# A row-wise logsumexp: nearly all row sums moved to VectorE, the late ones by halves, and a shorter first load

## The chip, the cores and the metric

The kernel runs on one core of a Trainium2 chip. The metric is device time in microseconds (us), the median of several executions.

## The reference

```python
# x: (32, 512, 1024) float32; axis: -1
def reference(x, axis):
    x_max = np.max(x, axis=axis, keepdims=True)
    return (x_max.squeeze(axis) + np.log(np.sum(np.exp(x - x_max), axis=axis))).astype(np.float32)
```

That is 16384 rows of 1024 numbers, 67.1 MB, each read once. The kernels leave out the maximum (the inputs are standard normal draws, so the exponentials do not overflow) and compute log(sum(exp(x))).

## The kernel before

Each of the 128 partitions gets 128 rows, which arrive in 17 loads into a ring of 51 rows. A "row" below means one row in every partition, 512 KB in all. ScalarE (ACT) takes the exponential. The sum of a row is made in one of two ways: VectorE (DVE) sums several rows after a large exponential, or ACT's own accumulator sums a single row. The list says how many rows each load has, and how many of them DVE sums.

```python
CHUNKS = [
    (4, 1), (15, 11), (16, 10), (16, 15), (16, 0), (14, 0), (12, 9), (9, 5), (7, 5), (5, 4),
    (4, 3), (3, 0), (2, 2), (2, 2), (1, 0), (1, 0), (1, 0),
]
RING_ROWS = 51
LN_AT = 5
# ...
    load(0)                          # issued ahead of the start barrier
    n_early = len(body.instructions)
# ...
    for i, (r, n_dve) in enumerate(CHUNKS):
        if i:
            load(i)                  # waits until the ring slots it overwrites are free
        # ...
        nc.scalar.wait_ge(landed[i], 16)
        if n_dve:
            nc.scalar.activation(out=ring[:, s : s + n_dve], in_=ring[:, s : s + n_dve], func=Exp
            ).then_inc(act_done, 1)
            # ...
            nc.vector.reduce_sum(out=sums[:, row : row + n_dve], in_=ring[:, s : s + n_dve], axis=AX
            ).then_inc(dve_done, 1)
        for j in range(n_dve, r):    # one row at a time, summed by ACT's accumulator
            nc.scalar.activation(out=ring[:, s + j], in_=ring[:, s + j], func=Exp,
                accum_out=sums[:, row + j : row + j + 1]).then_inc(act_done, 1)
        # ...
    take_logs(logged, NB, dves, acts)        # logarithm of the 61 sums still open
    nc.scalar.wait_ge(act_done, acts)
    nc.scalar.dma_start(out=out_v, in_=res).then_inc(stored, 16)
```

The softmax here doesn't subtract the row's maximum and nothing guards it: scores larger than these inputs give would overflow.

Of the kernel before, what the change touches and what calls it, by code (L numbers as in the profile page):

```python
# [1 line left out]

# [4 lines left out]



CHUNKS = [  # L10
    (4, 1), (15, 11), (16, 10), (16, 15), (16, 0), (14, 0), (12, 9), (9, 5), (7, 5), (5, 4),
    (4, 3), (3, 0), (2, 2), (2, 2), (1, 0), (1, 0), (1, 0),
]
RING_ROWS = 51

LN_AT = 5


@with_exitstack
def kernel(  # L20
    ctx: ExitStack,
    tc: tile.TileContext,
    x: bass.AP,
    axis: bass.AP,
    out: bass.AP,
):
    nc = tc.nc
    P = nc.NUM_PARTITIONS

    assert axis in (-1, len(x.shape) - 1), f"only last-axis reduction supported, got {axis}"  # L30

    x_flat = x.flatten_outer_dims()
    N, D = x_flat.shape
    assert N % P == 0
    NB = N // P
    assert sum(r for r, _ in CHUNKS) == NB

    fp32 = mybir.dt.float32
    Exp = mybir.ActivationFunctionType.Exp
    Ln = mybir.ActivationFunctionType.Ln  # L40
    AX = mybir.AxisListType.X

    x_v = x_flat.rearrange("(p t) d -> p t d", p=P)
    out_v = bass.AP(tensor=out.tensor, offset=out.offset, ap=[[NB, P], [1, NB]])

    ring = nc.alloc_sbuf_tensor("ring", [P, RING_ROWS, D], fp32).ap()
    sums = nc.alloc_sbuf_tensor("sums", [P, NB], fp32).ap()
    res = nc.alloc_sbuf_tensor("res", [P, NB], fp32).ap()

    landed = [nc.alloc_semaphore(f"landed{i}") for i in range(len(CHUNKS))]  # L50
    act_done = nc.alloc_semaphore("act_done")
    dve_done = nc.alloc_semaphore("dve_done")
    stored = nc.alloc_semaphore("stored")
    used = sorted(sem.num for sem in [*landed, act_done, dve_done])
    assert used == list(range(used[0], used[0] + len(used)))


    hook = nc.pop_inst_callback()
    symbolic, nc._always_lower_symbolic_ap = nc._always_lower_symbolic_ap, False


    place = []
    row = slot = 0
    for r, _ in CHUNKS:
        if slot + r > RING_ROWS:
            slot = 0
        place.append((slot, row))
        slot += r
        row += r



    busy = [(0, 0)] * RING_ROWS
    acts = dves = 0

    def load(i):
        (s, row), r = place[i], CHUNKS[i][0]
        act_wait = max(a for a, _ in busy[s : s + r])
        dve_wait = max(d for _, d in busy[s : s + r])
        if dve_wait:  # L80
            nc.sync.wait_ge(dve_done, dve_wait)
        if act_wait:
            nc.sync.wait_ge(act_done, act_wait)
        nc.sync.dma_start(out=ring[:, s : s + r], in_=x_v[:, row : row + r]).then_inc(
            landed[i], 16
        )

    def take_logs(lo, hi, dve_wait, act_wait):
        nonlocal acts
        nc.scalar.wait_ge(act_done, act_wait)  # L90
        nc.scalar.wait_ge(dve_done, dve_wait)
        nc.scalar.activation(out=res[:, lo:hi], in_=sums[:, lo:hi], func=Ln).then_inc(  # L92
            act_done, 1
        )
        acts += 1

    body = nc.main_func.blocks[-1]
    assert not body.instructions
    load(0)
    n_early = len(body.instructions)  # L100

    nc.scalar.preload_act_table_set("natural_log_exp_and_others")  # L102

    logged = 0
    done_before = [(0, 0)]
    for i, (r, n_dve) in enumerate(CHUNKS):
        if i:
            load(i)
        s, row = place[i]
        if i == LN_AT:  # L110
            logged = row
            take_logs(0, logged, *done_before[i])
        nc.scalar.wait_ge(landed[i], 16)
        if n_dve:
            nc.scalar.activation(  # L115
                out=ring[:, s : s + n_dve], in_=ring[:, s : s + n_dve], func=Exp
            ).then_inc(act_done, 1)
            acts += 1
            nc.vector.wait_ge(act_done, acts)
            nc.vector.reduce_sum(  # L120
                out=sums[:, row : row + n_dve], in_=ring[:, s : s + n_dve], axis=AX
            ).then_inc(dve_done, 1)
            dves += 1
            for j in range(n_dve):
                busy[s + j] = (0, dves)
        for j in range(n_dve, r):
            nc.scalar.activation(  # L127
                out=ring[:, s + j],
                in_=ring[:, s + j],
                func=Exp,  # L130
                accum_out=sums[:, row + j : row + j + 1],
            ).then_inc(act_done, 1)
            acts += 1
            busy[s + j] = (acts, 0)
        done_before.append((dves, acts))

    take_logs(logged, NB, dves, acts)
    nc.scalar.wait_ge(act_done, acts)
    nc.scalar.dma_start(out=out_v, in_=res).then_inc(stored, 16)


    nc.scalar.sem_clear(range(used[0], used[-1] + 1))


    first = nc.main_func.blocks[0]
    head, work = first.instructions, body.instructions
    end = next(k for k, i in enumerate(head) if i.opcode == "UnconditionalBranch")
    head, tail = head[:end], head[end:]
    for ins in work[:n_early]:
        at = next(  # L150
            k for k, i in enumerate(head) if i.engine == ins.engine and i.opcode == "Drain"
        )
        head.insert(at, ins)
    first.instructions = head + work[n_early:] + tail
    body.instructions = []

    nc._always_lower_symbolic_ap = symbolic
    nc.push_inst_callback(hook)


    tc.close()
    tc.compile()
    nc.gpsimd.wait_ge(stored, 16)
    nc.gpsimd.sem_inc(stored, -16)


# [1 line left out]
_INS = ['x', 'axis']  # L168
_OUTS = [((32, 512), 'float32')]

_NUMBERS = {'axis': -1}


# [26 lines left out]
```

## Time and profile before

| | before |
|---|---|
| time, median | 163.45 us |
| span of the profiled run | 161.4 us |
| ACT busy | 124.1 us (77%) |
| DVE busy | 72.9 us (45%) |
| share of 16 load engines taken by the loads | 97.0% |
| last share of the last load lands | 158.21 us |
| result stored | 161.35 us |

The first thing to ask of a table like this is whether the busiest resource has holes. ACT at 77% has them, ahead of each of the first five loads (until 83.84 us). The loads at 97% have none between the first packet and the last. The last two rows of the table are landing records of the trace: a load is carried by 16 engines, and counts as landed when the last of the 16 shares is in. Their difference, 3.14 us, is called the tail below. It holds the last exponential, the last logarithm and the store.

### The profile page before, as it was taken

How to read it: one execution, taken by the hardware profiler on the slowest of the kernel's cores; microseconds unless marked ns; L12 is line 12 of the kernel's file. 1: busy time of each engine (PE TensorE's matmuls, PEld its weight loads, DVE VectorE, ACT ScalarE, POOL GpSimd, SP SyncE). 2: the span in 40 equal slices, each digit the busy share in tenths (PEclk: the TensorE clock that was granted, in tenths of full speed). 3: DMA queues.
4: the chain of work that ended last, by engine and by line, in shares of the span. 5: the costliest groups of instructions: out<-in, count | busy, mean ns of one | idle time of the engine just before them, and what ended most of it. 6: DMA issues, size and time to landing. Idle time of an engine off the chain costs nothing.

```text
span 161.4 us, 212 instructions
## 1 busy us (share of the span) xinstructions
DVE 72.9 (45%) x11; ACT 124.1 (77%) x136; POOL 0.2 (0%) x4
## 2 busy tenths in 40 slices
DVE  0030000029960699000799920000004999799874
ACT  3190006997089980999429999999999999999995
POOL 0000000000000000000000000000000000000000
DMA  7999799989989989989989999999899999999990
GB/s 264 499 487 442 335 442 520 422 357 520 422 357 520 422 357 520 422 357 520 422 353 426 457 455 422 390 463 475 347 439 434 433 441 402 431 418 416 420 394 24
DMA packets 2593, 67.18 MB, mean 416 GB/s; under 512 B 288, under 2 KB 416, under 8 KB 800
## 3 DMA queue, kind: packets, MB, share of 16 engines
q1 hardware_dynamic: 2448, 67.11, 97.0%
q10 hardware_dynamic: 144, 0.07, 0.1%
q14 instruction: 1, 0.01, 0.0%
HBM read 67.11 MB, written 0.07 MB: 416 GB/s over the span
## 4 chain that ended last, share of the span: by engine, by line
ACT 52%; DMA 38%; DVE 7%; issue 1%
DMA ring<-in_x_dram 38%; ACT ring L127 30%; ACT ring L115 22%; DVE sums L120 7%; ACT res L92 0%
## 5 line engine op out<-in xcount | busy, mean ns | idle before, releaser
L120 DVE TENSOR_REDUCE sums<-ring 128x5 f32<-128x5120 f32 (+8 forms) x11 | 72.9, 6648 | 86.1 <-ACT ring L115 86.0
L115 ACT ACTIVATE ring<-ring 128x5120 f32<-128x5120 f32 (+8 forms) x11 | 59.3, 5395 | 29.6 <-DMA ring<-in_x_dram 29.6
L127 ACT ACTIVATE ring<-ring 128x1024 f32<-128x1024 f32 x61 | 63.4, 1041 | 5.3 <-DMA ring<-in_x_dram 5.3
L127 ACT ACTIVATION_READ_ACCUMULATOR ring<-ring 128x1 f32 x61 | 11.4, 187 | 0.0
L102 ACT ACT_TABLE_LOAD x1 | 1.3, 1283 | 0.8 <-PEq L181 0.8
L92 ACT ACTIVATE res<-sums 128x67 f32<-128x67 f32 (+1 forms) x2 | 0.5, 256 | 0.1
L181 POOL MEMSET const-bfloat16-1.0<- 128x1 bf16 x1 | 0.1, 101 | 0.0
L181 POOL MEMSET const-uint8-127<- 128x1 uint8 x1 | 0.1, 101 | 0.0
L181 POOL MEMSET const-float32-0.0<- 128x1 f32 x1 | 0.1, 98 | 0.2 <-issue 0.2
L181 POOL MEMSET const-float32-1.0<- 128x1 f32 x1 | 0.1, 98 | 0.0
## 6 DMA issues: line engine op xcount, KB each, us to landing
ring<-in_x_dram SPq DMA_DIRECT2D x1, 7680.0 KB, 24.9
ring<-in_x_dram SPq DMA_DIRECT2D x1, 7168.0 KB, 36.0
ring<-in_x_dram SPq DMA_DIRECT2D x1, 6144.0 KB, 21.6
ring<-in_x_dram SPq DMA_DIRECT2D x1, 4608.0 KB, 32.1
ring<-in_x_dram SPq DMA_DIRECT2D x2, 2048.0 KB, 26.3
ring<-in_x_dram SPq DMA_DIRECT2D x1, 3584.0 KB, 40.2
ring<-in_x_dram SPq DMA_DIRECT2D x1, 2560.0 KB, 44.4
ring<-in_x_dram SPq DMA_DIRECT2D x2, 1024.0 KB, 46.0
```

Of the source, the lines that this page charges most:

```text
L92: nc.scalar.activation(out=res[:, lo:hi], in_=sums[:, lo:hi], func=Ln).then_inc(act_done, 1)
L102: nc.scalar.preload_act_table_set("natural_log_exp_and_others")
L115: nc.scalar.activation(out=ring[:, s : s + n_dve], in_=ring[:, s : s + n_dve], func=Exp).then_inc(act_done, 1)
L120: nc.vector.reduce_sum(out=sums[:, row : row + n_dve], in_=ring[:, s : s + n_dve], axis=AX).then_inc(dve_done, 1)
L127: nc.scalar.activation(out=ring[:, s + j], in_=ring[:, s + j], func=Exp, accum_out=sums[:, row + j : row + j + 1],).then_inc(act_done, 1)
L181: nc = _bacc.Bacc("TRN2", target_bir_lowering=False, num_devices=1)
```

## The change

The intent was to take work off ACT. A row that ACT sums itself costs it about 0.19 us more than its part in a large exponential (1.04 us start to start against 0.853 in the trace before). DVE gets 119 of 128 rows instead of 67. To keep DVE from being late at the end, 15 late rows are summed by halves: one instruction adds the two halves of a row and accumulates the result, so it is an instruction of 512 columns instead of 1024. The last four rows keep ACT's accumulator, which now writes to a tensor in PSUM instead of SBUF, where the ring lies. The first load has two rows instead of four, and two loads are issued ahead of the barrier. The trace before shows one fetch of instructions inside the span (q14, 8192 bytes in 335 ns at 89.07 us); with fewer instructions on ACT, it was to go.

```diff
 CHUNKS = [
-    (4, 1), (15, 11), (16, 10), (16, 15), (16, 0), (14, 0), (12, 9), (9, 5), (7, 5), (5, 4),
-    (4, 3), (3, 0), (2, 2), (2, 2), (1, 0), (1, 0), (1, 0),
+    (2, 2, 1, False), (15, 15, 1, False), (14, 14, 1, False), (16, 16, 2, False),
+    (16, 16, 2, False), (14, 14, 2, False), (14, 11, 2, False), (10, 10, 2, False),
+    (8, 6, 1, False), (6, 6, 1, True), (4, 4, 1, True), (3, 3, 1, True), (2, 2, 1, True),
+    (1, 0, 1, False), (1, 0, 1, False), (1, 0, 1, False), (1, 0, 1, False),
 ]                                  # rows, rows for DVE, pieces, by halves
-LN_AT = 5
+LN_AT = 7
+LN_LAG = 1
+LATE = 4
 ...
+    late = nc.alloc_psum_tensor("late", [P, 512], fp32).ap()
 ...
     load(0)
+    load(1)
 ...
+        if i == len(CHUNKS) - 1:
+            take_logs(logged, late_row, sums[:, logged:late_row], *done_before[-LATE])
 ...
+            if by_halves:
+                for j in range(lo, hi):
+                    nc.vector.tensor_tensor_reduce(
+                        out=ring[:, s + j, : D // 2],
+                        in0=ring[:, s + j, : D // 2],
+                        in1=ring[:, s + j, D // 2 :],
+                        scale=1.0, scalar=0.0, op0=Add, op1=Add,
+                        accum_out=sums[:, row + j : row + j + 1],
+                    ).then_inc(dve_done, 1)
 ...
-                accum_out=sums[:, row + j : row + j + 1],
+                accum_out=total(row + j),          # PSUM for the last four rows
 ...
-    take_logs(logged, NB, dves, acts)
+    take_logs(late_row, NB, late[:, : NB - late_row], dves, acts)
```

More of the change, by code (lines that the diff above doesn't have):

```diff
@@ L35 @@
     NB = N // P
-    assert sum(r for r, _ in CHUNKS) == NB
+    assert sum(r for r, *_ in CHUNKS) == NB
     fp32 = mybir.dt.float32
@@ L40 @@
     Ln = mybir.ActivationFunctionType.Ln
+    Add = mybir.AluOpType.add
     AX = mybir.AxisListType.X
@@ L63 @@
     row = slot = 0
-    for r, _ in CHUNKS:
+    for r, *_ in CHUNKS:
         if slot + r > RING_ROWS:
@@ L74, with cuts @@
     acts = dves = 0
+    def cuts(n, parts):
+        ends = [-(-n * k // parts) for k in range(parts + 1)]
+        return [(lo, hi) for lo, hi in zip(ends, ends[1:]) if lo < hi]
     def load(i):
@@ L86, in load, with take_logs @@
         )
-    def take_logs(lo, hi, dve_wait, act_wait):
+    def take_logs(lo, hi, src, dve_wait, act_wait):
         nonlocal acts
@@ L91, in take_logs, with total @@
         nc.scalar.wait_ge(dve_done, dve_wait)
-        nc.scalar.activation(out=res[:, lo:hi], in_=sums[:, lo:hi], func=Ln).then_inc(
-            act_done, 1
-        )
+        nc.scalar.activation(out=res[:, lo:hi], in_=src, func=Ln).then_inc(act_done, 1)
         acts += 1
+    late_row = place[-LATE][1]
+    assert not any(n_dve for _, n_dve, _, _ in CHUNKS[-LATE:])
+    def total(t):
+        return late[:, t - late_row : t - late_row + 1] if t >= late_row else sums[:, t : t + 1]
     body = nc.main_func.blocks[-1]
@@ L105 @@
     done_before = [(0, 0)]
-    for i, (r, n_dve) in enumerate(CHUNKS):
-        if i:
+    for i, (r, n_dve, parts, by_halves) in enumerate(CHUNKS):
+        if i > 1:
             load(i)
@@ L110 @@
         if i == LN_AT:
-            logged = row
-            take_logs(0, logged, *done_before[i])
+            logged = place[i - LN_LAG][1]
+            take_logs(0, logged, sums[:, :logged], *done_before[i - LN_LAG])
+        if i == len(CHUNKS) - 1:
+            take_logs(logged, late_row, sums[:, logged:late_row], *done_before[-LATE])
         nc.scalar.wait_ge(landed[i], 16)
-        if n_dve:
+        for lo, hi in cuts(n_dve, parts):
             nc.scalar.activation(
-                out=ring[:, s : s + n_dve], in_=ring[:, s : s + n_dve], func=Exp
+                out=ring[:, s + lo : s + hi], in_=ring[:, s + lo : s + hi], func=Exp
             ).then_inc(act_done, 1)
@@ L119 @@
             nc.vector.wait_ge(act_done, acts)
-            nc.vector.reduce_sum(
-                out=sums[:, row : row + n_dve], in_=ring[:, s : s + n_dve], axis=AX
-            ).then_inc(dve_done, 1)
-            dves += 1
-            for j in range(n_dve):
-                busy[s + j] = (0, dves)
+            if by_halves:
[4 more added lines that the diff above has]
+                        in1=ring[:, s + j, D // 2 :],
+                        scale=1.0,
+                        scalar=0.0,
+                        op0=Add,
+                        op1=Add,
+                        accum_out=sums[:, row + j : row + j + 1],
+                    ).then_inc(dve_done, 1)
+                    dves += 1
+                    busy[s + j] = (0, dves)
+            else:
+                nc.vector.reduce_sum(
+                    out=sums[:, row + lo : row + hi], in_=ring[:, s + lo : s + hi], axis=AX
+                ).then_inc(dve_done, 1)
+                dves += 1
+                for j in range(lo, hi):
+                    busy[s + j] = (0, dves)
         for j in range(n_dve, r):
```

## The prediction

> **What bounds the kernel now.** I read the page's slices and DMA queues first, because a kernel that reads 67 MB once can end no earlier than its last byte.
>
> ```profile
> DMA  7999799989989989989989999999899999999990
> q1 hardware_dynamic: 2448, 67.11, 97.0%
> q14 instruction: 1, 0.01, 0.0%
> ```
>
> The load queue is busy from the second slice to the last but one, with no hole; q14 is one fetch of instructions. The windows of the last microseconds show when it stops (columns: stretch, length, DVE, ACT, POOL busy, clock, DMA share, GB/s):
>
> ```profile
> 156.00:157.00 1.00, 1.00 (x2) 1.00 (x2) 0.00 (x0) 1.00 1.01 406
> 157.00:158.00 1.00, 1.00 (x1) 1.00 (x3) 0.00 (x0) 1.00 0.32 127
> 158.00:159.00 1.00, 1.00 (x1) 1.00 (x3) 0.00 (x0) 1.00 0.00 0
> ```
>
> In the trace's landings the last of the 16 shares of the last load arrives at 158.21 us; call this T. Then the chain of waits (start, length, what):
>
> ```profile
> 0.78 24.87 DMA ring<-in_x_dram
> 25.67 9.60 ACT ring L115
> 35.29 11.90 DVE sums L120
> 47.21 36.61 DMA ring<-in_x_dram
> 83.84 10.56 ACT ring L127 x21
> ...
> 159.28 0.19 ACT ring L127
> 159.50 0.25 ACT res L92
> ```
>
> By shares it says ACT 52%, DMA 38%, which invites one to relieve ACT. That is the trap: the chain goes through ACT because ACT never pauses after 83.84, but the loads never pause either. The step through DVE at 35.29 is the release of a ring slot; the load that it frees is issued at 47.21 and the queue still holds 17 us of work. So two limits coincide: the stream ends at T, and ACT reaches the last row 0.13 us later (the last exponential starts at 158.34). After T come exponential and accumulator read (to 159.47), logarithm (to 159.75), store (161.35); the span is 161.4 us, and the time, 163.45 us, is 2.05 above it.
>
> The stream has a simple law. The trace gives the median packet (one partition's rows of a load) as 161 ns for 1 row, 311 for 2, 611 for 4, 2267 for 15, 2420 for 16. Each of 16 engines carries eight per load: 8 x 2267 ns = 18.14 us against 18.13 between the first two landings; 8 x 2420 = 19.36 against 19.36 between the next two but one. The line through them is 10.5 ns a packet plus 150.6 ns a row, so a load costs 0.084 + 1.205 us a row. Costs of the engines, by form:
>
> ```profile
> L115 ACT ACTIVATE ring<-ring 128x11264 f32<-128x11264 f32 x1 | 9.6, 9589 | 14.0 <-DMA ring<-in_x_dram 14.0
> L127 ACT ACTIVATE ring<-ring 128x1024 f32<-128x1024 f32 x61 | 63.4, 1041 | 5.3 <-DMA ring<-in_x_dram 5.3
> L127 ACT ACTIVATION_READ_ACCUMULATOR ring<-ring 128x1 f32 x61 | 11.4, 187 | 0.0
> L120 DVE TENSOR_REDUCE sums<-ring 128x11 f32<-128x11264 f32 x1 | 11.9, 11885 | 25.4 <-ACT ring L115 25.4
> ```
>
> Start to start, an exponential of n rows costs 0.853n + 0.10 us (25.67 to the next instruction at 35.17: 9.50), a row with its own accumulator 1.04 (8.50 to 9.54). A VectorE sum of n rows takes 1.067n + 0.15 (11.885), about 0.09 of it hidden behind the next one (two of 2.28 us merge to 4.48). All three stay under the stream's 1.21 us a row.
>
> [...]
>
> **The change, part by part.**
>
> *First load of two rows, second issued before the barrier.* The stream now starts at an effective 2.62 us (7.52 landed, less 8 x 0.611). It still carries 128 rows in 17 loads, so by the law it ends where it ended: 2.62 + 17 x 0.084 + 128 x 1.205 = 158.3. Two rows last 2.5 us, and the second load is queued before the first byte moves (packets begin at 1.00 us), so no hole opens. ACT starts at about 5.1 rather than 7.5, into idle time. Worth 0, give or take 0.2 us.
>
> *The rows move to VectorE.* ACT sheds the accumulator cost on 52 of 61 rows, some 52 x 0.19 = 10 us less work, all of it ahead of waits for loads. DVE gets 119 rows instead of 67. Does it return slots in time? The tightest is load 4, which reuses the slots of loads 0 and 1. Load 1 lands at 5.1 + 18.14 = 23.3; its exponential ends at 36.2, its sum (15 x 1.067 + 0.15) at 52.4. The stream runs dry at 23.3 + 16.95 + 19.36 = 59.6. Slack 7.2 us, and an issue needs about 1.0 (0.00 to 1.00). Stepping the same sums on, load 5 is released at 67.5 against 79.0, load 6 at 84.7 against 95.9, load 7 at 103.3 against 112.9, load 8 at 110.8 against 125.0; later loads have more. No hole.
>
> *Half sums late.* An estimate from the reduce's own fixed costs: 512/0.96 = 0.533, about 0.06 start to start[...]: 0.65 us instead of 1.067. On 15 rows that saves 6 us of DVE work. Whether it is needed is seen backward from T. Loads of 6, 4, 3, 2 rows land at T-16.3, T-11.3, T-7.7, T-5.2. Their exponentials end at T-11.0, T-7.5, T-4.8, T-3.0. DVE, which carries a small queue from load 6 (done 130.1, load 7 at 141.0, load 8 at 147.5, that is T-10.8), then needs 6 x 0.65 to T-6.9, 4 x 0.65 to T-4.3, 3 x 0.65 to T-2.3, 2 x 0.65 to about T-1.0.
>
> *The tail on ACT.* Four single rows land at T-3.9, T-2.6, T-1.3, T. ACT, free at T-3.0, needs 1.04 each: T-2.0, T-0.9, T+0.1; rounding and a late start of the chunks make this T+0.1 to T+0.3. The logarithm of 47 sums now comes here, about 0.2 start to start (100.60 to 100.79 in the mid one). So the last exponential starts near T+0.4, against T+0.13 before: +0.3. The final logarithm is of 4 values instead of 61, 57/1.2 = 47 ns less[...]. Store unchanged.
>
> *Instruction fetch.* One packet of 335 ns on one of 16 engines goes. The shares of a load landed 0.84 us apart before it (82.97 to 83.81) and 0.83 after (114.47 to 115.30), so it did not delay the slowest engine: 0.
>
> Sum: stream 0, tail +0.3 - 0.1 = +0.2. 163.45 + 0.2 = about 163.6 us.
>
> **The rivals.**
>
> *The half sums run at half rate.* 1024/0.96 + 0.12 = 1.19 us a row. From T-10.8, 15 rows end at T+7.1; the logarithm of 47 waits, and then exponential, logarithm and store follow: +7.2 us, 170.7. [...]Against it: [...]that halving would have no sense for whoever tuned this. At 0.80 us a row, by the same sum, DVE ends at T+1.2 and the time is some 164.8.
>
> *A wait on slots takes the place of ACT's load.* Whole sums free slots late (52.4 instead of 47.2 for load 4). The 7.2 us of slack speak against it; if DVE were slower than the reduce shows, each microsecond past 59.6 less an issue time would be one of the total.
>
> *Relieving ACT gains.* If the chain's 52% were what sets the end, 10 us less would give 154. The stream's end at T forbids it: even with ACT done at once, only 0.13 us of lag could go. The gain can be no more than that plus the fetch's 0.3, or 163.0.
>
> *A faster start.* If smaller first packets shorten the start (the first packets took 1.0 to 1.5 us instead of 0.61), the whole stream shifts, by up to perhaps 0.4: 163.1.
>
> **Range and chances.** Stream and start give 0.3 either way, the tail 0.2; a half sum of 0.70 to 0.80 adds up to 1.2. Range 162.9 to 164.6, with most of what is outside on the slow side. A gain of 2% needs 160.2, before the stream's end plus its tail: 1%. A loss of 2% needs 166.7, which only half rate or a hole in the stream gives: 9%. Within 2%: 90%.
>
> **What would show it.** The chain should become almost all DMA until its last 2 us; ACT idle ahead of every load until about 142; the last landing within 0.3 of 158.2; the half sum with its read near 0.65 us start to start; the DVE's last one ended before the logarithm of 47; the last exponential 0.3 to 0.5 after T; no instruction packet inside the span. I am wrong if the slices of the load queue show a hole, if a half sum takes over 0.72 (then DVE ends after the third single row), or if the last landing moves by more than 0.4.

Its sum came to 163.45 + 0.3 - 0.1 = about 163.6 us. Of the 0.1, 47 ns stand as an estimate: 57 columns of the last logarithm at 1.2 columns a ns, the rate of ACT's exponentials in the trace before (13.00 us for 15 rows, 1.90 for 2). The other 50 ns or so were a gain assumed for PSUM; the kernel before has no tensor there. Without it the sum is about 163.7.

The 0.65 us of a half sum came from 0.533 + 0.06 + a term of about 0.06 for reading the accumulator. The 0.96 columns a ns are the rate of the reduce in the trace before (16.15 us for 15 rows, 5.48 for 5), and the first 0.06 is its fixed 0.15 less the 0.09 hidden behind the next one. The 0.12 in the rival's 1.19 us is the sum of the same two terms. That a sum of two inputs keeps the rate of the reduce was the estimate, and half rate a guess against it: the trace before has no such instruction.

## The result, and the profile after

The changed kernel is correct and takes 163.34 us (163.19 to 163.75, six runs) against 163.45 us (163.22 to 163.53, six runs). The ratio is 0.9998, 95% interval 0.9985 to 1.0011: the same. A ratio here is the mean time of one kernel's fast runs over the mean of the other's fast runs of the same rounds, so it is not quite the ratio of the medians quoted.

ACT's work fell from 124.1 to 115.1 us, DVE's rose from 72.9 to 121.4, and the time did not move. The page's slices and queues after the change:

```profile
DMA  7999799999989989989999999999999999999990
q1 hardware_dynamic: 2448, 67.11, 96.9%
```

The stream of loads still has no hole, and the line for the fetch of instructions (q14) is gone. The windows around its end, with the columns of the prediction's fence:

```profile
156.00:157.00 1.00, 0.77 (x4) 1.00 (x3) 0.00 (x0) 1.00 0.99 397
157.00:158.00 1.00, 0.00 (x0) 1.00 (x3) 0.00 (x0) 1.00 0.23 90
158.00:159.00 1.00, 0.00 (x0) 1.00 (x4) 0.00 (x0) 1.00 0.00 0
```

The stream stops in the same microsecond as before. The last share lands at 158.17 us against 158.21, and the tail is 3.12 us against 3.14. DVE is idle from 156.77 on. The chain of waits (start, length, what):

```profile
0.42 22.91 DMA ring<-in_x_dram
...
36.39 16.17 DVE sums L155
...
52.58 26.41 DMA ring<-in_x_dram
...
158.22 0.24 ACT res L105
158.46 1.01 ACT ring L162 x2
...
159.50 0.17 ACT res L105
```

This chain misleads in the same way as the one before. It passes through a DVE sum of 16 us because that sum released a ring slot at 52.58. But the load released there landed only at 78.99, behind a queue that did not run dry until 59.64. Time in which a released load waits behind other loads is shown as if the release had mattered. The costs of the engines, by form (busy us, then mean ns of one):

```profile
L135 ACT ACTIVATE ring<-ring 128x8192 f32<-128x8192 f32 x4 | 27.9, 7022 | 12.6 <-DMA ring<-in_x_dram 12.6
...
L142 DVE CUSTOM_DVE_ANT_0 ring<-ring 128x512 f32<-128x512 f32 x15 | 9.3, 689 | 0.0
...
L142 DVE DVE_READ_ACCUMULATOR2_ANT sums<- 128x1 f32 x15 | 1.3, 84 | 0.0
```

And the end of the timeline (start, length, engine, line, instruction):

```profile
148.10 0.08 DVE L142 DVE_READ_ACCUMULATOR2_ANT sums<- 128x1 f32 x1
148.10 0.69 DVE L142 CUSTOM_DVE_ANT_0 ring<-ring 128x512 f32<-128x512 f32 x1
148.72 0.08 DVE L142 DVE_READ_ACCUMULATOR2_ANT sums<- 128x1 f32 x1
...
156.68 0.09 DVE L142 DVE_READ_ACCUMULATOR2_ANT sums<- 128x1 f32 x1
...
157.22 1.05 ACT L162 ACTIVATE ring<-ring 128x1024 f32<-128x1024 f32 x1
...
158.22 0.24 ACT L105 ACTIVATE res<-sums 128x47 f32<-128x47 f32 x1
158.35 1.05 ACT L162 ACTIVATE ring<-ring 128x1024 f32<-128x1024 f32 x1
159.30 0.17 ACT L162 ACTIVATION_READ_ACCUMULATOR ring<-ring 128x1 f32 x1
159.50 0.17 ACT L105 ACTIVATE res<-late 128x4 f32<-128x4 f32 x1
```

The reader should see three things. The read of the accumulator (84 ns) starts together with the next half sum (148.10), so it adds nothing, and a half sum costs about 0.61 us start to start. The DVE's last one is done at 156.77, 1.45 us before the logarithm of 47 sums. And that logarithm takes 0.13 us of ACT (158.22 to 158.35) just before the last exponential.

### The profile page after: what moved, and what is told of

It is laid out like the page before. It is cut to its first block, busy times and chain, and to the rows that moved or that the text cites. A ratio compares the mean times of both kernels' runs of the same rounds, so it can differ in the third digit from the quotient of the medians.

```text
span 161.3 us, 146 instructions
## 1 busy us (share of the span) xinstructions
DVE 121.4 (75%) x44; ACT 115.1 (71%) x40; POOL 0.2 (0%) x4
## 4 chain that ended last, share of the span: by engine, by line
DMA 45%; ACT 28%; DVE 25%; issue 0%; SPq 0%
DMA ring<-in_x_dram 45%; DVE sums L155 25%; ACT ring L135 24%; ACT ring L162 4%; ACT res L105 0%; SPq L97 0%
## 5 line engine op out<-in xcount | busy, mean ns | idle before, releaser
L155 DVE TENSOR_REDUCE sums<-ring 128x8 f32<-128x8192 f32 (+6 forms) x14 | 112.2, 8071 | 35.4 <-ACT ring L135 35.4
L135 ACT ACTIVATE ring<-ring 128x8192 f32<-128x8192 f32 (+8 forms) x18 | 104.3, 5837 | 43.3 <-DMA ring<-in_x_dram 43.3
L162 ACT ACTIVATE ring<-ring 128x1024 f32<-128x1024 f32 x9 | 9.3, 1043 | 0.0
L142 DVE CUSTOM_DVE_ANT_0 ring<-ring 128x512 f32<-128x512 f32 x15 | 9.3, 689 | 0.0
L162 ACT ACTIVATION_READ_ACCUMULATOR ring<-ring 128x1 f32 x9 | 1.6, 175 | 0.0
L142 DVE DVE_READ_ACCUMULATOR2_ANT sums<- 128x1 f32 x15 | 1.3, 84 | 0.0
L105 ACT ACTIVATE res<-sums 128x77 f32<-128x77 f32 (+1 forms) x2 | 0.5, 248 | 0.0
```

What stands on the lines that cost most here:

```text
L105: nc.scalar.activation(out=res[:, lo:hi], in_=src, func=Ln).then_inc(act_done, 1)
L135: nc.scalar.activation(out=ring[:, s + lo : s + hi], in_=ring[:, s + lo : s + hi], func=Exp).then_inc(act_done, 1)
L142: nc.vector.tensor_tensor_reduce(out=ring[:, s + j, : D // 2], in0=ring[:, s + j, : D // 2], in1=ring[:, s + j, D // 2 :], scale=1.0, scal ...
L155: nc.vector.reduce_sum(out=sums[:, row + lo : row + hi], in_=ring[:, s + lo : s + hi], axis=AX).then_inc(dve_done, 1)
```

## The experiments

The theory: the stream of loads fixes the end, ACT and DVE both lie beside it with known slack, and the small pieces of the tail cancel. The rivals: the engines set the pace (so relieving one should gain, or loading the other should cost at once), or slot waits or the start shape the stream. Nine kernels tell these apart, and two runs repeat. Each edit is against the changed kernel.

The table gathers the trace records on which the readings rest (us). It is worth more than the medians here: the first column shows what the stream does, the second how late the engines are at its end.

| run | last landing | tail | time, median |
|---|---|---|---|
| before | 158.21 | 3.14 | 163.45 |
| changed | 158.17 | 3.12 | 163.34 |
| e1_stream | 157.92 | 2.95 | 162.85 |
| e2_late_whole | 157.73 | 8.79 | 168.75 |
| e3_six_whole | 158.33 | 4.52 | 164.79 |
| e4_two_whole | 158.06 | 3.03 | 163.02 |
| e5_old_start | 157.94 | 3.11 | 163.16 |
| e6_fetch | 158.19 | 3.12 | 163.22 |
| e7_no_psum | 158.08 | 3.27 | 163.37 |
| e8_log_behind | 158.27 | 2.97 | 163.16 |
| e9_ring46 | 173.25 | 3.01 | 178.11 |
| e10_again | 158.35 | 3.10 | 163.39 |
| e11_behind_again | 157.78 | 2.98 | 162.75 |

### The stream alone

```diff
+        if i < len(CHUNKS) - LATE:      # no exponential, no sum
+            nc.vector.wait_ge(landed[i], 16)
+            nc.vector.tensor_tensor(out=sums[:, row : row + r], in0=ring[:, s : s + r, 0],
+                in1=ring[:, s : s + r, 0], op=mybir.AluOpType.mult).then_inc(dve_done, 1)
+            ...
+            continue
```

> The changed kernel's loads with almost no arithmetic: VectorE squares one element of each row (to release the ring slot), ScalarE does only the last four rows and the logarithms; the result is wrong on purpose. Theory (the stream of loads sets the end): the last landing stays at 158.2 us within 0.3, and only the 0.18 us by which ScalarE is late after it can go: 163.2 us, within 0.3% of the changed kernel. Rival (the engines' work, or their use of the buffer, slows the stream or sets the end): 5 us or more shorter, below 158.5.

Measured: 162.85 us (162.78 to 163.18), ratio to the kernel before 0.9962 (0.9947 to 0.9977); the result is wrong, as intended. From the page of this run:

```profile
DVE 2.3 (1%) x13; ACT 6.1 (4%) x11; POOL 0.2 (0%) x4
...
q1 hardware_dynamic: 2448, 67.11, 97.3%
```

The code cut leaves out one more thing: the two logarithms of these rows become one, of 124 sums, ahead of the last exponential. With 95% of ACT's time (6.1 left of 115.1 us) and 98% of DVE's (2.3 of 121.4) taken away, the loads end at 157.92 us, 0.25 earlier, and the tail is 0.17 shorter. That is 0.42 us together. The median is 0.49 us below that of the changed kernel, which was not run in these rounds; against the kernel before, in the same rounds, the gain is 0.6 us (ratio 0.9962). So about half a microsecond of 163 is all that the arithmetic ahead of the last four rows costs, and no other assignment of those rows to engines can gain more under these loads. (Other sizes and numbers of loads were not tried.) The time fell short of the expected 163.2 by 0.35: the tail part was foreseen, the 0.25 in the landing was not. It lies inside the scatter of the landings in the table. The rival (5 us or more) is out.

### Late sums whole

```diff
-    (6, 6, 1, True), (4, 4, 1, True), (3, 3, 1, True), (2, 2, 1, True),
+    (6, 6, 1, False), (4, 4, 1, False), (3, 3, 1, False), (2, 2, 1, False),
```

> The four late chunks of 6, 4, 3 and 2 rows are summed whole instead of by halves. Theory (half sums are needed by this assignment of rows): a late row costs 1.067 us instead of the 0.613 measured, so from 147.5 us VectorE ends near T+5.3 instead of T-1.4, the logarithm of 47 sums waits for it, and the time is 168.8 us, +5.5. Rival (the late sums lie beside the stream and are hidden anyway): within 0.5 us of the changed kernel.

Measured: 168.75 us (168.44 to 168.94), ratio 1.0317 (1.0300 to 1.0333). From its timeline:

```profile
163.46 0.24 ACT L105 ACTIVATE res<-sums 128x47 f32<-128x47 f32 x1 [5.59 <-DVE sums L155]
```

The stream ended at 157.73 and ACT then stood 5.59 us before the logarithm of 47 sums. So with nearly all rows on DVE the half sums are not a refinement: without them the change loses 3%.

### Only the six-row chunk whole, only the two-row chunk whole

```diff
-    (6, 6, 1, True),
+    (6, 6, 1, False),          # e3_six_whole
-    (2, 2, 1, True),
+    (2, 2, 1, False),          # e4_two_whole
```

> Only the chunk of 6 rows is summed whole, those of 4, 3 and 2 by halves. Theory: 6 x 0.454 = 2.7 us more VectorE work on a chain that has no pause from 147.5 us on and 1.4 us of slack before the logarithm of 47 sums: VectorE ends near T+1.1, and the time grows by about 1.2 us to 164.6. Rival (slack is larger, or the work before was waiting for ScalarE): no change.

> Only the last VectorE chunk of 2 rows is summed whole. Theory: 2 x 0.454 = 0.9 us more, less than the 1.4 us of slack: VectorE ends near T-0.6 and the time stays at 163.3 within 0.3. Rival (every microsecond on VectorE late counts): +0.9 us, 164.3.

Measured: 164.79 us (164.71 to 164.99), ratio 1.0079 (1.0062 to 1.0096), for the six rows; 163.02 us (162.88 to 163.08), ratio 0.9967 (0.9952 to 0.9982), for the two. The logarithm of 47 sums in the timeline of the six-row run:

```profile
159.79 0.24 ACT L105 ACTIVATE res<-sums 128x47 f32<-128x47 f32 x1 [1.31 <-DVE sums L142]
```

The last sum and the logarithm of 47 sums in that of the two-row run:

```profile
155.21 2.28 DVE L155 TENSOR_REDUCE sums<-ring 128x2 f32<-128x2048 f32 x1
...
158.03 0.23 ACT L105 ACTIVATE res<-sums 128x47 f32<-128x47 f32 x1
```

Six whole sums add 2.7 us to a DVE chain with 1.45 us of slack, and ACT waits 1.31. Two add 0.9 us; DVE ends at 157.49 (155.21 + 2.28) and the logarithm starts at 158.03 without a wait. The slack is thus bracketed from both sides. The two-row run is even a little below the kernel before, and only 0.17 us above the stream alone in the same rounds. Its landing (158.06) lies 0.11 us below that of the changed kernel, which is inside the scatter described under the repeats. Its tail (3.03 instead of 3.12) has an account in the traces. In both runs ACT does not pause between the landing of the six-row load (141.81 here, 142.01 in the changed kernel) and the last exponential, and the result is stored 19.28 and 19.27 us after that landing. But here the last load landed 16.25 us after the six-row load instead of 16.16. So the tail is what ACT's unbroken work leaves over when the last load is in: a stream that is slower by 0.09 us at the end shortens the tail by as much. At the very end ACT is thus not beside the path but 0.1 to 0.2 us behind the stream.

### The old start

```diff
-    (2, 2, 1, False), (15, 15, 1, False),
+    (4, 4, 1, False), (13, 13, 1, False),
...
-    load(1)                    # no longer ahead of the barrier
```

> The start of the kernel before put back into the changed one: first load of 4 rows (then 13 instead of 15), and only it issued ahead of the barrier. Theory (same bytes, same number of loads): the last landing stays within 0.3 us of 158.2 and the time within 0.3 us of 163.3. Rival (a shorter first load starts the stream sooner, by the 0.28 us seen in the first landing less its own packets): the last landing and the time grow by 0.3 us or more.

Measured: 163.16 us (162.97 to 163.54), ratio to the kernel before 0.9992 (0.9979 to 1.0005); last landing 157.94, tail 3.11. The start was worth nothing that can be seen. In the changed kernel two rows landed at 4.82, which is 2.34 after taking off their 8 packets of 309 to 311 ns each, against 2.63 by the same sum before (the prediction has 2.62); but the second load then took 18.52 us instead of 18.13. Some of its packets took up to 2762 ns instead of 2267, but slow packets are no mark of the short first load: in the repeat of the same program the second load took 18.19 us, and before the slowest took 2628. The 17 rows of the first two loads were in at 23.34 us in the changed kernel and at 23.12 here, and between 22.88 and 23.29 in the other runs with the new start.

### The second fetch of instructions

```diff
+        if i == 0:
+            pad = nc.alloc_sbuf_tensor("pad", [P, 128], fp32).ap()
+            nc.scalar.wait_ge(act_done, acts)
+            for k in range(100):
+                nc.scalar.activation(out=pad[:, k : k + 1], in_=ring[:, s, :1], func=Exp)
```

> A hundred tiny exponentials (one column each) on ScalarE after the first chunk, where it waits for the second load anyway[...]. Theory: an instruction packet of 8192 bytes shows inside the span, takes about 0.33 us of one of 16 load engines, and the time stays within 0.3 us of 163.3; some 10 us of ScalarE work are hidden too. Rival (the fetch delays the stream or ScalarE): the last landing or the time is later by 0.3 us or more.

Measured: 163.22 us (163.00 to 163.44), ratio 0.9988 (0.9976 to 1.0000). The page counts 246 instructions, against 146 in the changed kernel and 212 before. The queues on the page of this run show that the fetch is back:

```profile
q14 instruction: 1, 0.01, 0.0%
```

The trace has it at 15.4 us, 8192 bytes in 309 ns. Last landing (158.19) and tail (3.12) are those of the changed kernel. The hundred extra instructions shortened ACT's wait for the second load from 16.6 to 7.0 us, so 9.6 us of ACT work were hidden as well: about what the change had saved. The fetch was not on the path. Nor was the ACT work put into the wait ahead of the second load; the run does not test whether ACT's late work, which the change also lightened, could come back unnoticed.

### Accumulators in SBUF again

```diff
-    late = nc.alloc_psum_tensor("late", [P, 512], fp32).ap()
+    late = nc.alloc_sbuf_tensor("late", [P, 512], fp32).ap()
```

> The accumulators of the last four rows go to SBUF instead of PSUM. Theory: each single row costs 1.04 us again instead of 1.00 start to start and the last logarithm reads SBUF; as ScalarE has no pause in this stretch, the last exponential starts about 0.12 later and the last logarithm about 0.2 to 0.3 later against the last landing: 163.6 us. Rival (destination makes no difference): the same instruction times as in the changed kernel.

Measured: 163.37 us (163.26 to 163.53), ratio 0.9998 (0.9986 to 1.0010). The time does not tell, the tail does: 3.27 us against 3.12 and 3.10 in the two profiles of the changed kernel. In its timeline:

```profile
157.21 1.04 ACT L162 ACTIVATE ring<-ring 128x1024 f32<-128x1024 f32 x1
...
158.25 0.23 ACT L105 ACTIVATE res<-sums 128x47 f32<-128x47 f32 x1
158.38 1.04 ACT L162 ACTIVATE ring<-ring 128x1024 f32<-128x1024 f32 x1
...
159.54 0.21 ACT L105 ACTIVATE res<-late 128x4 f32<-128x4 f32 x1
```

A single row before the logarithm costs 1.04 us (157.21 to 158.25) instead of 1.00 (157.22 to 158.22 in the changed kernel), and the last logarithm 0.21 instead of 0.17. The last exponential starts 0.30 us after the last landing instead of 0.18, the 0.12 that were expected. PSUM is worth 0.15 us in the tail, less than the 0.2 to 0.3 expected.

### The logarithm of 47 sums behind the last exponential

```diff
-        if i == len(CHUNKS) - 1:
-            take_logs(logged, late_row, sums[:, logged:late_row], *done_before[-LATE])
...
+    rows_done = acts
+    take_logs(logged, late_row, sums[:, logged:late_row], dves, done_before[-LATE - 1][1])
-    take_logs(late_row, NB, late[:, : NB - late_row], dves, acts)
+    take_logs(late_row, NB, late[:, : NB - late_row], dves, rows_done)
```

> The logarithm of the 47 sums is put behind the last exponential instead of ahead of it. Theory: it then runs in the 0.17 us in which ScalarE waits for the last accumulator, and the last exponential starts 0.13 us earlier, T+0.05: 163.2 us, a gain of about 0.1 that timing alone will hardly show. Rival (the logarithm delays the last one by as much as it delayed the exponential): no change against the last landing.

Measured: correct, 163.16 us (162.88 to 163.40), ratio to the kernel before 0.9986 (0.9974 to 0.9998). In its timeline:

```profile
158.31 1.06 ACT L160 ACTIVATE ring<-ring 128x1024 f32<-128x1024 f32 x1
159.26 0.17 ACT L160 ACTIVATION_READ_ACCUMULATOR ring<-ring 128x1 f32 x1
159.31 0.25 ACT L105 ACTIVATE res<-sums 128x47 f32<-128x47 f32 x1
159.46 0.17 ACT L105 ACTIVATE res<-late 128x4 f32<-128x4 f32 x1
```

The last exponential starts 0.04 us after the last landing (158.31 less 158.27) instead of 0.18, and the logarithm fills the gap in which ACT had waited for the accumulator. The tail is 2.97 us, 0.15 less. With almost no arithmetic (e1_stream) it was 2.95, so this is nearly all that could be had there.

### A ring that is too short

```diff
-RING_ROWS = 51
+RING_ROWS = 46
```

> The ring shortened from 51 to 46 rows, so that the fourth load (16 rows) no longer has free slots of its own and must wait for the whole sum of the 15-row chunk. Theory (whole sums return slots late, and the kernel is spared only because the ring is long enough): the load is released at 52.5 us, its first packets move about 1 us later, and the stream, dry since 40.3, has one hole of 13 us; everything after shifts by it and the time is 176.6 us. Rival (the wait is absorbed by later slack): within 2% of 163.3.

Measured: 178.11 us (178.03 to 178.18, two runs), ratio 1.0902. The slices of the load engines, and what they moved:

```profile
DMA  9998899950009988999889999999899999999991
GB/s 461 390 446 376 375 520 442 455 221 0 0 0 476 431 372 387 476 476 476 387 379 442 429 481 442 442 416 416 357 446 446 387 446 401 424 420 415 414 421 46
```

There is the hole that the prediction's second rival would have made, and the whole time shifts by it. It is larger than expected. The load was issued at 52.20 us, once the 15-row sum had ended; its first packets began at 53.16 but took 2.9 to 3.5 us instead of 2.42, and on the 16 engines they began over 0.44 us. It landed at 74.31, which is 2.76 us more than the issue and its own 19.35 us. So filling the empty queue cost 2.8 us here and not the 1.0 that I had put in, which is only the time to the first packet. The prediction's own 2.62 us from the first issue to the effective start of the stream is a cost of the same size, and could have warned me. The missing 1.5 us of the expectation are the 1.8 between the two, less 0.3 for an earlier release.

### The repeats

Both kernels unaltered: the changed one, and the one with the logarithm behind, in the same rounds on one chip.

> The changed kernel once more, unaltered, on the chip and in the rounds of the next one. Theory: the last landing wanders by some 0.3 us between profiles of the same loads (157.7 to 158.3 so far), while the stretch from the last landing to the stored result repeats at 3.12 us within 0.03; time 163.3, not distinguishable from the kernel before. Rival (the difference in the last landing belongs to the kernel): the last landing is again 158.17 within 0.05.

> The version with the logarithm of 47 sums behind the last exponential, once more, beside the changed kernel on one chip. Theory: 2.97 us from the last landing to the stored result, 0.15 less than the changed kernel's; the time 0.15 us below it, which five rounds may or may not separate. Rival (the earlier 0.3 us in the median against the kernel before was a real gain of this version): 0.3 us below the changed kernel in the same rounds.

Measured: 163.39 us (162.75 to 163.45) for the changed kernel, ratio to the kernel before 0.9992 (0.9972 to 1.0012); 162.75 us (162.60 to 163.26) for the other, ratio 0.9965 (0.9947 to 0.9983). The tails repeat, 3.10 against 3.12, and 2.98 against 2.97. The last landings do not: 158.35 against 158.17 for the same program, and 157.78 against 158.27 for the other. Over all runs with these loads and no hole they lie between 157.73 and 158.35, with no relation to what the engines did that I can see.

So moving the logarithm gains 0.12 to 0.15 us by the traces, which is shown. In the first series it was 0.14% below the kernel before, in the second 0.35%, and in the second 0.64 us below the changed kernel's median. Most of that is a difference in the last landing (157.78 against 158.35 in the profiles). It arose early: the eight-row load landed at 134.33 in the one and 134.85 in the other, 0.52 apart, and up to there the two programs give the same instructions in the same order. So in these two profiles the order of the logarithms did not make it. The runs without a profile cannot be split in this way, and the rival of that expectation, a real gain of 0.3 us, is not excluded. By these rounds this version is the fastest of the three, by less than half a per cent.

## Why the prediction was right

The forecast was 163.6 us with 90% for no change beyond 2%; it came out at 163.34. Point by point:

- **The stream ends where it ended.** Right. Landing 158.17 against 158.21, and the packet law held (8 x 2418 ns for 16 rows is 19.34, and 19.34 and 19.35 were seen). The stream alone shows that it is the floor. The agreement to 0.04 us is luck: the same program landed at 158.35 in its repeat.
- **Relief of ACT is worth nothing.** Right: nearly all work taken away gains about 0.5 us. The 9.6 us put back cost nothing either, but that tests only ACT's wait ahead of the second load.
- **The half sum costs 0.65 us.** Right in kind, 0.04 too dear: about 0.613. The estimate had a term of 0.06 for the accumulator read, but the read, 84 ns long, starts with the next half sum. DVE therefore ended at T-1.4 and not T-1.0. The main rival, half rate (1.19 us a row), is out.
- **Slots come free in time.** Right, with a wrong margin. The release at 52.4 was measured as 52.58, the queue running dry at 59.6 as 59.64. But the issue into an empty queue took 2.8 us in the run with the short ring, not 1.0, so the real margin, as an estimate from that run, was about 4.3 us (59.64 - 52.58 - 2.76) and not 6.
- **The tail grows by 0.2.** Wrong by 0.2. The last exponential started 0.18 us after the landing, not 0.4: the logarithm of 47 took 0.13 and not 0.2, and each row into PSUM cost 0.04 less, which adds up over a stretch in which ACT never pauses. From the start of the last exponential to the stored result it took 2.94 us instead of 3.01, so 0.07 of the forecast's 0.1 came. The tail is 3.12 instead of 3.34, and this is nearly the whole difference between 163.6 and 163.34.
- **The start and the fetch are worth 0.** Right, each undone by itself.
- **The signs I gave.** Three were wrong. The chain did not become almost all DMA: it reads DMA 45%, ACT 28%, DVE 25%, since it follows slot releases that nobody was waiting for yet. I had named this trap and then used the same view as a test. The last exponential started 0.18 us after the last landing, not 0.3 to 0.5. And ACT was not idle ahead of every load until about 142: it had no pause ahead of the ten-row load (landed 124.99), was last idle at 134.73, for 0.16 us, and was busy from then on.

## What to carry to other kernels

When one queue has no hole from its first byte to its last, count the time after its end and the time before its start (3.14 and 2.63 us in the kernel before); what can be reduced is those, and what the queue carries. Do not take the shares of the chain of waits for the bound where loads are queued far ahead: compare the moment at which a slot is released with the moment at which the queue runs dry, and allow for filling it again (2.76 us here). Half sums and the like are then worth what they save in slack (here 0.45 us a row, 1.067 less 0.613), which can be measured by undoing them one chunk at a time.
